# Mixer of a two-layer fp32 trunk: v by seven block products between the pieces of u, the head norm in 512-column operations, the norm of v queued early

## The chip, the cores and the metric

The kernel runs on one core of a Trainium2 chip. The core has a matrix engine (PE), three engines for elementwise work (DVE, ACT, POOL), queues for DMA transfers (SP's queue issues most of them, POOL's the accumulating ones), on-chip memory for operands and a second on-chip memory of banks into which PE accumulates. The metric is the device time of one execution in microseconds; lower is better.

## What is computed

```python
for l in range(2):                                    # D = 1024, T = 256 tokens, all in fp32
    x = LN(alpha * x + 0.5 * swiglu_1(x))
    u, v, q, k, val, gates = split(x @ w_in[l])
    u, v = gelu(u), gelu(v)                           # exact gelu
    h_a = u * spatial(LN(v))                          # per channel group: 128x128 causal mixing of positions, + bias
    o   = (softmax(q1 k1) - lam * softmax(q2 k2)) val # differential attention, 8 heads, rotary q and k
    h_b = rms_norm_per_head(o) * (1 - lam_init)
    m   = sigmoid(g_A) * (h_a @ w_branch[0]) + sigmoid(g_B) * (h_b @ w_branch[1])
    x = LN(alpha * x + m @ w_out)
    x = LN(alpha * x + 0.5 * swiglu_2(x))
```

## The kernel before

**Products in three parts.** A tile is 128 partitions wide, so the 256 tokens are two token tiles and D is eight steps of 128. Each fp32 factor is split into a high part (rounded, written by ACT) and a low part (the factor less its high part, written by DVE), and each product is three matmuls: high by high, high by low, low by high. The names are `whi`/`wlo` for weights, `xh`/`xl` (`x_cat`) for activations, `hb` for the attention's output. `stream` (L195 the high part, L197 the low) fetches a megabyte of weights through SP into one of four raw buffers and splits it in pieces of 128x1024; each piece lives in one of eight high and one of eight low buffers. `pieces`/`split` (L247, L249) do the same for data that is already there. `gemm_b` and `gemm_b2` give token rows, 512 columns a matmul (L283); `gemm_a2` gives channel rows (L295 for the high weights, 512 wide, L302 for the low ones, 256 wide), and DVE joins its two halves (L303 on ACT, L305 or L307 on DVE).

**Seven products.** In the FFN a product of 2x2 blocks is done by seven block products in place of eight (the Strassen-Winograd scheme). This needs sums of blocks of x (`strassen_sums`) and sums of weight blocks: `plus` adds two weight blocks on DVE (L359), `gather` adds a block to one in memory by an accumulating DMA from POOL's queue (L353), `homes` is a pair of the eight weight buffers used as landing place, and `product` issues the twelve matmuls of one block product (four steps of 128, three parts each, L376).

**The mixer.** In each layer, in PE's order: val (`gemm_b2`), four pairs of q and k with the rotary turn, the attention of head pair 0 to 3 (`attend`, strung in between as tasks), the gates by rows and by columns twice, `u_part((0, 1))` (two megabytes of u's weights, one 512-column gelu each), v (`gemm_b` twice, 96 matmuls of L283), `u_part((2, 3))`, the branch of `hb` (`branch_rows(1, hb)`), the spatial mixing (`spatial`, L1169), the branch of `ha`, and the output product.

At the end of `attend`, PE multiplies by val (L1049, L1051), ACT copies the bank (`on`, L1054) and sums the squares of each of four head rows (L1059), POOL works out four reciprocal roots in a chain of fifteen small operations (L1062, then `rsqrt4`, L268 to L276), ACT scales the four pieces (L1068), POOL separates the two 16-bit planes (L216) for a transposing DMA, DVE joins them (L229), and ACT and DVE write `hb`'s two parts (L1083, L1085).

v's chunks pass a gelu (ACT L1136) and `bn_stats` (DVE L1137); `settle` aggregates (L1142), takes a reciprocal root on DVE (`rsqrt`, L255 to L261) and normalizes `vg` in two operations for each half (L1146, L1148).

**What sets the order.** PE's order is the order in which the program is written. For the other engines a scheduler sorts by a priority that goes up with every fetch (`step`), so that an operation runs in the order of the fetches around it unless `soon()` lowers its number or `behind` names an instruction after which it has to be issued. Tasks (`beside(task, delay)`) are taken up after a delay counted in pieces of PE work (`beat`). `line` holds an engine's instructions to the order in which they were written, where it is set. Each engine then carries out its list strictly in order: an instruction that waits holds up all behind it.

## Time and profile before

| | |
|---|---|
| three timed runs | 1186.97, 1187.22, 1188.16 us (median 1187.22) |
| profiled execution, its own time | 1187.5 us |
| its span (first to last instruction) | 1185.8 us |
| PE / DVE / ACT / POOL busy | 1180.3 / 1013.8 / 827.9 / 280.1 us |
| granted PE clock | 1.0 throughout |

The profile has a page (busy time by engine, slices, the chain of work that ended last, the costliest groups), and the trace behind it answers with a timeline, with busy time by stretch, with waits and with groups of instructions. Rows read: start in us, duration in us, engine, line of the program, operation, output<-input, and in brackets the time for which the engine stood idle before, with what released it. Times in the text for the stage of interest are of layer 0; layer 1 shows the same rows 586.7 us later.

### The profile page before, as it was taken

What the parts mean: (1) busy time and instruction counts of PE and PEld (TensorE: products, weight loads), DVE (VectorE), ACT (ScalarE), POOL (GpSimd) and SP (SyncE); (2) the same over time, 40 slices, a digit from 0 to 9 for tenths busy, and PEclk for the clock granted to TensorE, in tenths of its full rate; (3) what the DMA queues carried; (4) which work ended last, traced back from release to release, by engine and by line L of the source; (5) the groups of instructions that cost most, each with busy time, mean ns of one, the idle gap of its engine ahead of it and who ended that gap; (6) DMA issues with size and microseconds to landing.
All of it is one profiled execution on the core that took longest, in us unless ns stands there. A gap on an engine that the chain in (4) does not pass through costs nothing.

```text
span 1185.8 us, 16672 instructions
## 1 busy us (share of the span) xinstructions
PE 1180.3 (100%) x5775; PEld 994.8 (84%) x5775; DVE 1013.8 (85%) x1559; ACT 827.9 (70%) x1418; POOL 280.1 (24%) x352
## 2 busy tenths in 40 slices
PE   9999999999999999999999999999999999999998
PEld 8888888888888888888888888888888888888887
DVE  6989989888688989889899889888965989988895
ACT  6688658559855667876567876666788556679761
POOL 1011201247420220051020141004564012102600
PEclk9999999999999999999999999999999999999999
DMA  9969976767865658689668689586666755786881
GB/s 351 260 207 262 288 272 210 264 191 239 244 210 169 225 187 273 188 275 275 229 224 262 194 274 277 198 293 231 215 203 204 255 178 172 256 247 211 271 256 36
DMA packets 129620, 275.10 MB, mean 232 GB/s; under 512 B 89040, under 2 KB 90368, under 8 KB 105472
## 3 DMA queue, kind: packets, MB, share of 16 engines
q1 hardware_dynamic: 121968, 248.67, 63.5%
q0 software_dynamic: 6992, 24.71, 8.8%
q8 instruction: 45, 0.74, 0.3%
q10 hardware_dynamic: 576, 0.66, 0.2%
q14 instruction: 39, 0.32, 0.1%
HBM read 248.05 MB, written 1.05 MB: 210 GB/s over the span
## 4 chain that ended last, share of the span: by engine, by line
PE 99%; DMA 0%; DVE 0%; ACT 0%; DVEq 0%; issue 0%
PE bank L283 46%; PE bank L295 15%; PE sbank L376 12%; PE bank L410 10%; PE bank L302 8%; PE sbank L410 3%; PE bank L521 2%; PE sbank L995 1%; PE bank L376 1%; PE sbank L1051 1%; PE sbank L1169 1%; DMA xtok<-in_xT 0%; PE sbank L1049 0%; PE sbank L692 0%; DVE xtok L679 0%; ACT whi L247 0%
## 5 line engine op out<-in xcount | busy, mean ns | idle before, releaser
L197 DVE TENSOR_TENSOR wlo<-raw,whi 128x1024 fp32r<-128x1024 f32 (+1 forms) x346 | 379.7, 1124 | 50.9 <-ACT whi L195 37.9
L195 ACT ACTIVATE whi<-raw 128x1024 fp32r<-128x1024 f32 (+1 forms) x350 | 323.2, 952 | 134.8 <-PE bank L283 43.5
L283 PE MATMUL bank<-whi,x 128*128 128x512 f32 x1224 | 386.3, 390 | 0.0
L283 PEld LDWEIGHTS bank<-whi,x 128*128 128x128 f32 x1224 | 229.9, 188 | 47.4
L283 PE MATMUL bank<-wlo,x 128*128 128x512 f32 x612 | 238.4, 390 | 0.0
L249 DVE TENSOR_TENSOR wlo<-raw,whi 128x1024 fp32r<-128x1024 f32 (+1 forms) x124 | 144.3, 1189 | 19.8 <-ACT whi L247 11.2
L247 ACT ACTIVATE whi<-raw 128x1024 fp32r<-128x1024 f32 (+1 forms) x124 | 121.6, 999 | 50.5 <-DVE raw L359 19.2
L295 PE MATMUL bank<-x,whi 128*128 128x512 f32 x640 | 153.3, 391 | 0.0
L295 PEld LDWEIGHTS bank<-x,whi 128*128 128x128 f32 x640 | 118.2, 188 | 23.7
L283 PEld LDWEIGHTS bank<-wlo,x 128*128 128x128 f32 x612 | 115.0, 188 | 23.4
L229 POOL COPY seven<-seven 128x512 uint16<-128x512 uint16 x16 | 51.9, 3299 | 139.3 <-DMA seven<-seven 80.2
L302 PEld LDWEIGHTS bank<-x,wlo 128*128 128x128 f32 x640 | 81.4, 191 | 2.9
L302 PE MATMUL bank<-x,wlo 128*128 128x256 f32 x640 | 82.6, 283 | 0.0
L410 PE MATMUL bank<-whi,hhi 128*128 128x512 f32 (+1 forms) x182 | 68.2, 375 | 0.0
L410 PE MATMUL bank<-whi,hlo 128*128 128x512 f32 (+1 forms) x182 | 67.9, 373 | 0.0
L410 PE MATMUL bank<-wlo,hhi 128*128 128x512 f32 (+1 forms) x182 | 67.9, 373 | 0.0
L971 POOL TENSOR_TENSOR swap<-swap,sin_t 128x512 f32<-128x512 f32 x16 | 28.7, 1792 | 100.9 <-DMA swap<-z 52.3
L735 POOL COPY nvia<-ntwo 128x256 uint16<-128x256 uint16 x20 | 9.9, 541 | 162.2 <-DMA ntwo<-nvia 115.2
L303 ACT ACTIVATE r<-bank 128x256 f32<-128x256 f32 x96 | 34.8, 372 | 16.2 <-PE bank L302 16.0
L376 PE MATMUL sbank<-whi,xhs 128*128 128x512 f32 x128 | 42.0, 389 | 0.0
L410 PEld LDWEIGHTS bank<-whi,hlo 128*128 128x128 f32 x182 | 34.3, 188 | 6.1
L410 PEld LDWEIGHTS bank<-wlo,hhi 128*128 128x128 f32 x182 | 34.3, 189 | 6.0
(283 smaller groups left out, 2153.5 us busy)
## 6 DMA issues: line engine op xcount, KB each, us to landing
raw<-in_w13b SPq DMA_DIRECT2D x68, 1024.0 KB, 5.7
raw<-in_w SPq DMA_DIRECT2D x32, 1024.0 KB, 7.0
raw<-in_wb SPq DMA_DIRECT2D x16, 1024.0 KB, 5.4
raw<-in_wqk SPq DMA_DIRECT2D x16, 1024.0 KB, 5.9
home<-in_w13b SPq DMA_DIRECT2D x16, 512.0 KB, 5.9
raw<-in_w13a SPq DMA_DIRECT2D x8, 1024.0 KB, 5.0
home<-in_w SPq DMA_DIRECT2D x16, 512.0 KB, 4.5
raw<-in_wgr SPq DMA_DIRECT2D x8, 1024.0 KB, 5.4
```

The source lines that it names most:

```text
L195: inline(A, A.activation(h, r, AF.Copy).ins)
L197: low = eng.tensor_tensor(out=w, in0=r, in1=h.bitcast(F32), op=ALU.subtract).ins
L229: eng.tensor_copy(out=o, in_=i)
L247: a = A.activation(hi, src, AF.Copy).ins
L249: return a, eng.tensor_tensor(out=lo, in0=src, in1=hi.bitcast(F32), op=ALU.subtract).ins
L283: PE.matmul(ps, xx, w, start=start and n == 0, stop=stop and n == 2)
L295: PE.matmul(b[-1], hi[:, k * P : (k + 1) * P], xc(k), start=k == 0, stop=False)
L302: PE.matmul(b[n][:, :T], lo[:, k * P : (k + 1) * P], xc(k)[:, :T], start=False, stop=k == KT - 1)
L303: emptied[0] = A.activation(r[:, s], b[n][:, T:], AF.Copy, scale=scale).ins
L376: PE.matmul(ps, x[o](k), y, start=start and k == n == 0, stop=stop and k == 3 and n == 2, skip_group_check=True)
L410: PE.matmul(q[c][t][:, :n] if o == 0 else more[:, :n], x(k, t), y, start=k == 8 and m == 0 and (c, t) != (1, 0), stop=k == FT - 1 and m == ...
L971: turned_by[0] = G.tensor_tensor(out=s3, in0=s3, in1=s, op=ALU.mult).ins
```

## The change

```diff
+        x_sums = []                                            # right after val's product
+        wide = [[p.tile([P, HC], F32R, tag=n, name=name("xhs")) for p, n in ((hi_pool, "hi"), (lo_pool, "lo"))] for _ in range(2)]
+        made = [[v[:, n % 2 * 512 : n % 2 * 512 + 512] for v in wide[n // 2]] for n in range(4)]
+        for _ in strassen_sums(x_sums, made, *(norm.rows[v] for v in ((0, 0), (1, 0), (0, 1), (1, 1)))):
+            pass
...
-            for q in range(4):                                 # attend: the norm of a head pair
-                A.activation(d1[:, s], on[:, s], AF.Square, accum_out=ss[:, q : q + 1])
+            A.activation(d1, on, AF.Square)
+            with behind(added[0]):
+                V.tensor_reduce(out=ss, in_=d1.rearrange("p (q c) -> p q c", q=4), op=ALU.add, axis=AX.X)
...
-            for q in range(4):
-                with behind(emptied[0]):
-                    A.activation(on[:, s], on[:, s], AF.Copy, scale=r[:, q : q + 1])
+            with behind(added[0]):
+                V.tensor_tensor(out=on4, in0=on4, in1=r.unsqueeze(2).to_broadcast([P, 4, P]), op=ALU.mult)
...
-        u_part((0, 1))
-        for h in range(2):
-            gemm_b(wb[l, V_, h], KT, xh, xl, got_v)            # 2 x 48 matmuls
+        def seven():
+            r1 = fetch(w11); p1 = pieces(r1)
+            r4 = fetch(w21); p2 = pieces(r4)
+            product(bx, x11, p1, True, False)
+            product(bq, x12, p2, True, True)
+            A.activation(cross, bx, AF.Copy)
+            r2 = fetch(w12, raw=homes(hi_pool, "hi"))
+            yield
+            product(bz, x_sums[0], pieces(plus(r1, r2)), True, False)
+            gather(r2, w22)
+            r3 = fetch(w22, raw=homes(lo_pool, "lo"))
+            V.tensor_tensor(out=vg[0][:, 0], in0=bq, in1=cross, op=ALU.add)
+            got_v(0, 0)
+            A.activation(vg[1][:, 1], bz, AF.Copy)
+            yield
+            p1 = pieces(plus(r1, r3)); p2 = pieces(r3)
+            product(bx, x_sums[1], p1, False, False)
+            A.activation(vg[0][:, 1], bx, AF.Copy)
+            product(bz, x_sums[3], p2, False, True)
+            product(bx, x_sums[2], pieces(r2), False, False)
+            plus(r1, r4)
+            V.tensor_tensor(out=vg[0][:, 1], in0=bz, in1=vg[0][:, 1], op=ALU.subtract)
+            got_v(0, 1)
+            yield
+            p1 = pieces(r1)
+            V.tensor_tensor(out=vg[1][:, 1], in0=vg[1][:, 1], in1=bx, op=ALU.subtract)
+            got_v(1, 1)
+            product(bx, x22, p1, False, True)
+            got_v(1, 0, bx)
+            yield
+        line[:] = None, None, True
+        products = seven()
+        for gp in range(GROUPS // 2):
+            u_part((gp,))
+            next(products)
+        line[:] = None, None, False
...
         def settle():                                          # the same operations, in one go
+            with soon():
...
-        beside(settle(), 2.6)
+        beside(settle(), 0.4)
         for gp in range(GROUPS // 2):
-            beside(spatial(gp), 7.4 + 1.1 * gp)
-        u_part((2, 3))
+            beside(spatial(gp), 4.2 + 1.1 * gp)
```

v is done by seven products of a quarter of the weights (84 matmuls in place of 96) that stand between the four pieces of u: u0, w11, w21, u1, the sum w11+w12, u2, three products, u3, the last product. Three sums of weights are made by DVE and one by an accumulating DMA. The sums of x are made straight after val's product into two high and two low weight buffers, which they hold until v is done. The head norm's squares become one ACT operation and one reduction on DVE, its scaling one DVE operation, behind which the engine waits for POOL's roots. `settle` is queued early and without breaks.

How the lists move, at three places (numbers behind names count the tiles; the ones of the two kernels differ). DVE, where u0's product is done and the first v weights came before; the names are `hb`, the attention output, `onT`, its transposed planes, and `nwy`, POOL's roots:

```order
L305 TENSOR_TENSOR u_3080<-bank_3091,r_3127 128x256 [waits Activation_49]
L305 TENSOR_TENSOR u_3080<-bank_3118,r_3127 128x256 [waits Activation_49]
L197 TENSOR_TENSOR wlo_3368<-raw_3361,whi_3367 128x1024
L197 TENSOR_TENSOR wlo_3404<-raw_3401,whi_3403 128x1024 [waits DMAHW2_49,PE_49,Activation_49]
L305 TENSOR_TENSOR u_3172<-bank_3183,r_3202 128x256 [waits Activation_49]
L305 TENSOR_TENSOR u_3172<-bank_3192,r_3202 128x256 [waits Activation_49]
```

```order
L305 TENSOR_TENSOR u_3090<-bank_3101,r_3135 128x256 [waits DMAHW7_49,Activation_49]
L305 TENSOR_TENSOR u_3090<-bank_3126,r_3135 128x256 [waits Activation_49]
L229 COPY onT_3053<-on_2850 128x512 [waits DMAHW3_49,DVE_49,Pool_49]
L229 COPY onT_3053<-on_2850 128x512
L1076 TENSOR_TENSOR on_3117<-on_3117,nwy_3164 128x512 [waits Pool_49]
L197 TENSOR_TENSOR wlo_3238<-raw_3235,whi_3237 128x1024 [waits DMAHW7_49,Activation_49]
L197 TENSOR_TENSOR wlo_3242<-raw_3235,whi_3241 128x1024 [waits Activation_49]
L1093 SCALAR_TENSOR_TENSOR hb_1946<-onT_3053,dgs,hb_1946 128x256 [waits Activation_49]
L1093 SCALAR_TENSOR_TENSOR hb_1947<-onT_3053,dgs,hb_1947 128x256 [waits Activation_49]
L359 TENSOR_TENSOR raw_3184<-raw_3184,home_3230 128x1024 [waits DMAHW4_49]
L359 TENSOR_TENSOR raw_3184<-raw_3184,home_3231 128x1024 [waits DMAHW5_49]
```

Before, u1's last low piece (wlo_3368; its first stands ahead of these rows) and v's first one (wlo_3404) follow u0's join at once; now the pieces of v's first two products stand ahead of these rows, the scaling that waits for POOL's roots stands between, and behind it u1's low pieces (wlo_3238, wlo_3242) and the first sum of weights.

ACT, at the same place:

```order
L1054 ACTIVATE on_3107<-sbank_3100 128x512 [waits PE_49]
L1059 ACTIVATE d_2729,ss_3109<-on_3107 128x128 [waits Activation_49]
L1059 ACTIVATE d_2729,ss_3109<-on_3107 128x128 x3
L195 ACTIVATE whi_3367<-raw_3361 128x1024 [waits PE_49]
L303 ACTIVATE r_3127<-bank_3091 128x256 [waits PE_49]
L303 ACTIVATE r_3127<-bank_3118 128x256 [waits PE_49]
L1129 ACT_TABLE_LOAD
L1129 ACTIVATE u_3080<-u_3080 128x512 [waits DVE_49]
```

```order
L1063 ACTIVATE on_3117<-sbank_3110 128x512 [waits PE_49]
L1066 ACTIVATE d_2743<-on_3117 128x512 [waits Activation_49]
L303 ACTIVATE r_3135<-bank_3101 128x256 [waits PE_49]
L303 ACTIVATE r_3135<-bank_3126 128x256 [waits PE_49]
L1052 ACTIVATE aT_2972<-d_2970 128x512 [waits DMAHW2_49,Pool_49]
L1052 ACTIVATE aT_2972<-d_2970 128x512
L1137 ACT_TABLE_LOAD
L1137 ACTIVATE u_3090<-u_3090 128x512 [waits DVE_49]
L1159 ACTIVATE cross_3183<-sbank_3180 128x512 [waits PE_49]
L195 ACTIVATE whi_3237<-raw_3235 128x1024 [waits DMAHW7_49]
L195 ACTIVATE whi_3241<-raw_3235 128x1024
```

u1's high pieces (both done before u0's gelu in the first list) now come behind u0's gelu and the copy of the first v product.

DVE at the end of the stage, up to the first low piece of `branch_rows(1, hb)` (wlo_3705 before, wlo_3604 now):

```order
L229 COPY onT_3427<-on_3304 128x512
L1148 SCALAR_TENSOR_TENSOR vg_3224<-vg_3224,nwy_3553,bc_3077 128x512 [waits DMASW1_49,DVE_49]
L1085 SCALAR_TENSOR_TENSOR hb_1934<-onT_3427,dgs,hb_1934 128x256 [waits Activation_49]
L1085 SCALAR_TENSOR_TENSOR hb_1935<-onT_3427,dgs,hb_1935 128x256 [waits Activation_49]
L1148 SCALAR_TENSOR_TENSOR vg_3224<-vg_3224,nwy_3553,bc_3077 128x512
L261 TENSOR_SCALAR nwy_3636<-nwa_3635,yi_3632 128x1
L197 TENSOR_TENSOR wlo_3705<-raw_3702,whi_3704 128x1024 [waits DMAHW2_49]
```

```order
L249 TENSOR_TENSOR wlo_3555<-raw_3184,whi_3554 128x1024
L261 TENSOR_SCALAR nwy_3639<-nwa_3638,nwy_3635 128x1 [waits DVE_49]
L1180 TENSOR_TENSOR vg_3087<-vg_3087,sbank_3180 128x512
L260 TENSOR_SCALAR nwa_3642<-nwy_3639,ve_3630 128x1 [waits DVE_49]
L229 COPY onT_3467<-on_3325 128x512 [waits DMAHW3_49,Pool_49]
L261 TENSOR_SCALAR nwy_3643<-nwa_3642,nwy_3639 128x1 [waits DVE_49]
L229 COPY onT_3467<-on_3325 128x512
L1204 SCALAR_TENSOR_TENSOR vg_3086<-vg_3086,nwy_3643,bc_3083 128x512 [waits DMASW1_49,DVE_49]
L1204 SCALAR_TENSOR_TENSOR vg_3086<-vg_3086,nwy_3643,bc_3083 128x512
L1151 BN_STATS vst_3089<-vg_3087 128x6 [waits Activation_49]
L1093 SCALAR_TENSOR_TENSOR hb_1950<-onT_3467,dgs,hb_1950 128x256 [waits Activation_49]
L1093 SCALAR_TENSOR_TENSOR hb_1951<-onT_3467,dgs,hb_1951 128x256 [waits Activation_49]
```

The next row of the changed list is wlo_3604. Between wlo_3238 and wlo_3604, both counted, the changed list has 60 instructions: 17 low pieces, 6 halves of sums of weights, 6 halves of u, 6 of `hb`, 3 sums into `vg`, one reduction, one scaling, 3 `bn_stats`, 4 copies of `onT`, and `settle` for the first token tile (13).

64 lines of the change are left out of this document (38 added, 26 removed).

## Prediction

> **What bounds the kernel now.** First the page's busy times and the waits of PE, the engine that is busy throughout:
>
> ```profile
> PE 1180.3 (100%) x5775; PEld 994.8 (84%) x5775; DVE 1013.8 (85%) x1559; ACT 827.9 (70%) x1418; POOL 280.1 (24%) x352
> PE sbank L533 <- DVE warm L529: 1.0, 1, 1.0
> PE sbank L671 <- ACT minus L669: 0.7, 1, 0.7
> PE bank L521 <- ACT whi L247: 0.3, 1, 0.3
> ```
>
> PE waits 2.0 us in all: the kernel is as long as its matmuls, and one matmul less is time gained, as long as the others still deliver in time. So the question is their slack in the stage that changes, u and v. The chain of waits gives PE's part of it, the table by stretches DVE's (the columns are stretch and length, then busy us and instructions of PE, weight loads, DVE, ACT and POOL, clock, DMA share, GB/s):
>
> ```profile
> 300.56 1.84 PE bank L295 x8
> ...
> 307.49 3.65 PE bank L295 x16
> ...
> 313.05 6.83 PE bank L283 x30
> ...
> 321.22 14.98 PE bank L283 x66
> ...
> 347.30 9.55 PE bank L283 x42
> 300.00:310.00 10.00, 10.00 (x61) 8.89 (x60) 7.30 (x10) 9.94 (x24) 3.63 (x7) 1.00 1.10 281
> 310.00:320.00 10.00, 10.00 (x55) 8.61 (x54) 6.08 (x9) 9.23 (x18) 4.31 (x13) 1.00 0.75 280
> 320.00:330.00 10.00, 10.00 (x51) 8.47 (x51) 5.08 (x9) 5.35 (x17) 4.33 (x15) 1.00 0.45 138
> 330.00:340.00 10.00, 10.00 (x47) 8.32 (x46) 8.79 (x15) 7.79 (x11) 3.99 (x7) 1.00 0.69 159
> 340.00:350.00 10.00, 10.00 (x60) 8.87 (x59) 10.00 (x27) 5.57 (x11) 0.84 (x1) 1.00 0.70 290
> ```
>
> The stage runs from 300.6 (u0) to 347.3, where the branch of `hb` begins. DVE is busy 37.3 of the 50 us, and fully so in the last ten. It has some 13 us to give.
>
> **The change part by part.**
>
> *PE.* The 96 matmuls of v take 6.83 + 14.98 = 21.81 us, 0.227 each. Seven products need 84: 12 x 0.227 = 2.73 us less in each layer, 5.5 us in all. Were nothing late, the branch would begin at 344.6.
>
> *DVE's additions.* Six more low pieces, six halves of weight sums, three sums into `vg`, two reductions and two scalings fall into the stage. The prices:
>
> ```profile
> 202.85 5.76 DVE L197 TENSOR_TENSOR wlo<-raw,whi 128x1024 fp32r<-128x1024 f32 x5
> 208.53 0.75 DVE L307 SCALAR_TENSOR_TENSOR z<-bank,r 128x256 f32<-128x256 f32 x2
> L359 DVE TENSOR_TENSOR raw<-raw,home 128x1024 f32<-128x1024 f32 x32 | 38.5, 1217 | 0.0
> L305 DVE TENSOR_TENSOR u<-bank,r 128x256 f32<-128x256 f32 x16 | 6.3, 417 | 0.4 <-ACT r L303 0.4
> L229 DVE COPY onT<-on 128x512 uint16<-128x512 uint16 x16 | 6.4, 455 | 1.5 <-DMA on<-onT 1.5
> L1085 DVE SCALAR_TENSOR_TENSOR hb<-onT,dgs,hb 128x256 fp32r<-128x256 f32 x16 | 8.2, 550 | 6.8 <-ACT hb L1083 6.8
> L1137 DVE BATCH_NORM_STATS2 vst<-vg 128x6 f32<-128x512 f32 x8 | 5.5, 690 | 7.8 <-ACT vg L1136 7.8
> L1146 DVE SCALAR_TENSOR_TENSOR vg<-vg,mv,bc 128x512 f32<-128x512 f32 x8 | 6.1, 767 | 0.0
> L843 DVE TENSOR_TENSOR held<-held,held 128x512 f32<-128x512 f32 x16 | 11.0, 686 | 0.0
> L260 DVE TENSOR_SCALAR nwa<-nwy,ve 128x1 f32<-128x1 f32 x28 | 7.6, 272 | 0.7
> ```
>
> Back to back, five low pieces take 208.53 - 202.85 = 5.68, 1.14 each against 1.22 from start to end: neighbours overlap by 0.08, which I take off every mean. A half of a sum has the same mean (1.217), so 1.14 too; a 512-column sum costs 0.61. The reduction and the scaling have no row; between half of a 512-column operation (0.34) and a whole one with its end (0.69) I take 0.6. The additions are 12 x 1.14 + 3 x 0.61 + 4 x 0.6 = 17.9 us, more than the 13 that are free, and `settle`, which before ran on past 350, now falls into the stage for its first token tile. DVE becomes the bound here.
>
> *How long it holds up the branch.* `branch_rows(1, hb)` cannot go past its first matmul without wlo_3604. DVE reaches it after 60 instructions from wlo_3238 on: 23 of 1.14 (26.2), six halves of u at 0.34 (2.0), six of `hb` at 0.47 (2.8), three sums (1.8), reduction and scaling (1.2), three `bn_stats` at 0.61 (1.8), four copies at 0.38 (1.5), four normalizations at 0.69 (2.8), nine small ones at 0.06 to 0.2 (1.2). Sum 41.3 us. When does it begin? wlo_3238 needs its high piece from ACT:
>
> ```profile
> 304.93 0.58 ACT L1054 ACTIVATE on<-sbank 128x512 f32<-128x512 f32 x1
> 307.68 0.62 ACT L303 ACTIVATE r<-bank 128x256 f32<-128x256 f32 x2
> 308.32 1.28 ACT L1129 ACT_TABLE_LOAD   x1
> 309.62 0.63 ACT L1129 ACTIVATE u<-u 128x512 f32<-128x512 f32 x1
> 313.37 1.43 ACT L1043 ACTIVATE aT<-d 128x512 uint16<-128x512 uint16 x2
> L195 ACT ACTIVATE whi<-raw 128x1024 fp32r<-128x1024 f32 x268 | 275.6, 1052 | 86.2 <-PE bank L295 30.8 <-PE bank L283 23.4 <-PE bank L410 9.5
> ```
>
> In the new order these come after u0's last matmul (u1 begins at 307.5, as before): r until about 308.0, `aT` 1.4, table 1.3, gelu 0.5, the copy `cross` 0.5, the high piece 1.05: 312.7. The other wait ahead of it, for POOL's roots, ends earlier, as below. DVE has next to nothing to do from 308.5 until then. 312.7 + 41.3 = 354.0. Against that stands the matmul that first reads such a low piece:
>
> ```profile
> 347.37 0.40 PE L283 MATMUL bank<-wlo,hb 128*128 128x512 f32 x1
> ```
>
> It comes 354.0 - 347.4 = 6.6 us later, although PE had 2.7 us less to do.
>
> *POOL's chain.* The last head pair's scaling on DVE waits for fifteen small POOL operations, and these fare badly beside a busy DVE:
>
> ```profile
> 327.66 0.20 POOL L273 TENSOR_TENSOR nwa<-nwy 128x4 f32<-128x4 f32 x1
> 327.93 0.20 POOL L274 TENSOR_TENSOR nwa<-nwa,ve 128x4 f32<-128x4 f32 x1
> 1091.86 15.07 POOL L229 COPY seven<-seven 128x512 uint16<-128x512 uint16 x1
> 1093.58 4.63 DVE L197 TENSOR_TENSOR wlo<-raw,whi 128x1024 fp32r<-128x1024 f32 x4
> 1106.67 1.28 DVE L249 TENSOR_TENSOR wlo<-raw,whi 128x1024 fp32r<-128x1024 f32 x1 [0.37 <-ACT whi L247]
> ```
>
> Undisturbed, an operation of the chain follows the one before by 0.28 us, fifteen in 4.2. But a POOL copy begun while DVE went from one sum of two arrays to the next took 15.07 us and ended at 1106.9, just past DVE's first gap (1106.3 to 1106.67). For the first chain here DVE mostly idles, hence no delay to the 312.7. For the second one DVE has ten operations (about 9 us) between reduction and scaling; POOL gets on during `bn_stats`, u's two halves and the copies, some 2.4 us or eight operations, and DVE then stands for the other seven: 7 x 0.28 = 2.0 us. Bounds: 0 (all fifteen pass) and 4.2. The Trainium skill, "SBUF — State Buffer", section "Who interferes with whom", states that a DVE instruction with two SBUF inputs shuts out a GpSimd one that reads SBUF for its whole length; the row of 15.07 us agrees. The rule speaks against this change: without it the term would be 0.
>
> *Behind the stage.* The second token tile's `settle` now follows wlo_3604 and the pieces behind it, and the spatial matmuls of `ha` come within 10 us. Bounds 0 and 1.5 us from the four normalizations (2.8) against 1.2 us of slack; I take 0.5.
>
> *At nothing.* The sums of x are eight DVE operations of 0.61 (4.9 us) ahead of q's first low pieces, which are read by the first L302 of q:
>
> ```profile
> 199.44 2.36 DVE L197 TENSOR_TENSOR wlo<-raw,whi 128x1024 fp32r<-128x1024 f32 x2
> 206.04 1.91 PE bank L302 x16
> ```
>
> The first piece was done at 199.44 + 1.22 = 200.7 and is now by 205.6 at the latest, 0.4 before 206.0. If that cover fails it costs up to 1 us in each layer. The four weight buffers that they hold lower the run ahead from eight pieces to six; the gate stage, where DVE has idle time, covers that. SP and POOL issue four transfers more each; DMA's share of its engines is 0.45 to 0.75 from 310 on, where they fall. ACT gains six high pieces and loses the short operations of the head norm; it was busy 5.4 and 7.8 of 10 us between 320 and 340, so but for its order it is not the bound.
>
> **Sum.** For each layer 6.6 + 2.0 + 0.5 = 9.1 us, and both layers have the same lists: 18.2. From the profiled execution's own 1187.5 (span 1185.8 and 1.7 around it; the median of the runs is 1187.22) that makes 1205.7; as the terms' bounds leave more room below, I say 1205. By bounds: 6.6 less 2 if all rows shrink by 5%, no wait for POOL, nothing behind: 4.6, so 1197; and 6.6 + 4.2 + 1.5 = 12.3, so 1212.
>
> **The rivals.**
>
> *DVE keeps up and PE stays the bound:* 1187.5 - 5.5 = 1182. For it: DVE idles 13 us of 50, and before 300 it can run ahead. Against: from wlo_3238 the 41 us would have to fit into the 32 from 312.7 to 344.6, each row 22% shorter. Only if that piece could start at 303 would it fit, and ACT's list forbids that.
>
> *DVE loses only what it has too much of:* if ACT's pieces come some 5 us sooner (table and `aT` copies out of the way) and POOL does not hold it up, the branch starts at 348 to 350: +1 to +3 for each layer, 1189 to 1194. For it: ACT is full from 300 to 310 (9.94 of 10), and the head norm takes some of that away. Against: its order, in which the six instructions ahead of the piece all depend on u0's end.
>
> *POOL starves DVE further:* the transposed planes of the last head pair pass through two POOL copies while DVE is full. If one of them waits 15 us as at 1091.86, the transfer and the join behind it (a DVE row before wlo_3604) come some 5 to 6 us late: 1205 + 11 = 1216. Against: `bn_stats` and the sums from banks leave POOL two openings there.
>
> **How the numbers follow.** The main case 0.62, with 1197 to 1212 as its own range; PE-bound 0.10; the small loss 0.13; the starved POOL 0.15. About 0.2% (2.4 us) is what a measurement can tell from no change. Faster: the PE-bound case and a little of other errors, 0.11. Same: the lower edge of the small loss, 0.04. Slower 0.85. Leaving out the PE-bound case and the end of the starved one, the range is 1188 to 1214.
>
> **What would show it.** In the changed profile PE should wait about 11 to 12 us in each layer between 330 and 365, mostly for DVE's low pieces, the longest wait (5 to 9 us) at the start of the branch of `hb`; DVE should be busy without a gap from about 313 to 355, but for about 2 us before the last scaling, released by POOL; and between 308 and 313 it should stand for ACT. PE's busy time should be 5.5 us lower. I am wrong if PE's waits are at other stages, if DVE has gaps in that stretch, or if wlo_3604 is in time.

## The result, and the profile after

| | before | after |
|---|---|---|
| median of four runs each, on the same chip | 1187.51 us | 1214.69 us |
| from to | 1186.97 to 1188.16 | 1213.55 to 1215.99 |
| ratio | | 1.0228, 95% interval 1.0216 to 1.0241 |
| profiled execution / span | 1187.5 / 1185.8 | 1215.7 / 1213.9 |

The change makes the kernel 27 us slower. The forecast was 1205 with a range up to 1214, so the sign held, and the loss was larger than the range allowed, by 0.7 us. The profiled execution, 1215.7 us, lies 1.0 above the median. The page's busy times of the changed kernel:

```profile
PE 1186.8 (98%) x5751; PEld 993.5 (82%) x5751; DVE 1067.2 (88%) x1621; ACT 831.4 (68%) x1356; POOL 307.0 (25%) x356
```

PE has 24 matmuls fewer (5.5 us) and is yet busy 6.5 us longer. The lower clock below accounts for about 5 of these 12 us (an estimate: PE's busy time in the slow stretches of both layers, times the share of the clock that is missing there); the rest was not traced. Its waits (engine, output, line, what it waited for; us in total, times, longest):

```profile
PE sbank L376 <- DVE wlo L249: 8.8, 8, 2.1
PE sbank L376 <- DVE vg L1180: 4.8, 1, 4.8
PE sbank L376 <- ACT whi L195: 4.1, 1, 4.1
PE bank L283 <- DVE wlo L197: 1.7, 3, 0.8
...
PE sbank L1058 <- issue: 1.0, 1, 1.0
...
PE bank L283 <- DVE gz L305: 0.5, 1, 0.5
```

The first four rows are the new stage in both layers (19.4 us), where there was nothing before. The third row is layer 1's counterpart of the second: the profile names ACT there, but in both layers PE goes on 0.15 us after the same subtraction of DVE (L1180) has ended, at 356.17 and at 955.56. Busy time by stretch in layer 0 (columns as in the prediction):

```profile
300.00:310.00 10.00, 10.00 (x65) 9.03 (x64) 8.33 (x12) 7.52 (x17) 6.59 (x6) 1.00 0.81 161
310.00:320.00 10.00, 10.00 (x50) 8.38 (x49) 6.59 (x11) 7.81 (x14) 3.51 (x15) 1.00 0.41 124
320.00:330.00 10.00, 8.42 (x48) 6.78 (x47) 9.36 (x11) 7.20 (x11) 3.35 (x5) 1.00 0.99 278
330.00:340.00 10.00, 9.69 (x50) 7.71 (x48) 8.49 (x12) 8.63 (x13) 8.75 (x15) 1.00 0.78 164
340.00:350.00 10.00, 7.21 (x33) 5.74 (x34) 10.00 (x11) 5.82 (x7) 5.10 (x7) 1.00 0.60 131
350.00:360.00 10.00, 5.15 (x21) 4.20 (x21) 9.17 (x22) 6.25 (x10) 1.50 (x1) 0.75 0.85 310
```

From 320 on DVE is busy nearly throughout, and PE, which was busy throughout before, falls to 5.15 of 10 us. DVE's list in the timeline, from the scaling ahead of wlo_3238 (the first low piece of u1) to wlo_3604 (the first one of the branch of `hb`, the first half of the row at 361.02):

```profile
315.59 0.69 DVE L1076 TENSOR_TENSOR on<-on,nwy 128x512 f32<-128x512 f32 x1 [3.25 <-POOL nwy L276]
316.20 2.36 DVE L197 TENSOR_TENSOR wlo<-raw,whi 128x1024 fp32r<-128x1024 f32 x2
...
323.50 1.90 DVE L249 TENSOR_TENSOR wlo<-raw,whi 128x1024 fp32r<-128x1024 f32 x1
...
328.86 0.69 DVE L1068 TENSOR_REDUCE ss<-d 128x4 f32<-128x512 f32 x1 [0.59 <-ACT d L1066]
...
339.94 0.69 DVE L1076 TENSOR_TENSOR on<-on,nwy 128x512 f32<-128x512 f32 x1 [1.51 <-POOL nwy L276]
...
341.69 1.58 DVE L1093 SCALAR_TENSOR_TENSOR hb<-onT,dgs,hb 128x256 fp32r<-128x256 f32 x2
...
351.39 1.06 DVE L1202 SCALAR_TENSOR_TENSOR vg<-vg,mv,bc 128x512 f32<-128x512 f32 x1
...
358.87 0.69 DVE L1151 BATCH_NORM_STATS2 vst<-vg 128x6 f32<-128x512 f32 x1 [0.39 <-ACT vg L1150]
360.22 0.89 DVE L1093 SCALAR_TENSOR_TENSOR hb<-onT,dgs,hb 128x256 fp32r<-128x256 f32 x2 [0.65 <-ACT hb L1091]
361.02 2.35 DVE L197 TENSOR_TENSOR wlo<-raw,whi 128x1024 fp32r<-128x1024 f32 x2
```

Three rows are longer than their kind elsewhere: a low piece takes 1.90 in place of 1.22, two operations of `hb` 1.58 in place of 0.88, a normalization 1.06 in place of 0.74. Two of these three share their time with a copy of POOL (L216), the third with POOL's operation on `wsT`:

```profile
315.36 0.20 POOL L276 TENSOR_TENSOR nwy<-nwa,nwy 128x4 f32<-128x4 f32 x1
...
322.81 1.50 POOL L216 COPY onT<-on 128x512 uint16<-128x512 uint16 x2
329.63 1.10 POOL L1071 TENSOR_TENSOR ss<-s,ss 128x4 f32<-128x4 f32 x1 [5.32 <-DVE ss L1068]
...
339.71 0.20 POOL L276 TENSOR_TENSOR nwy<-nwa,nwy 128x4 f32<-128x4 f32 x1
340.77 2.23 POOL L216 COPY onT<-on 128x512 uint16<-128x512 uint16 x2 [0.86 <-DVE on L1076]
...
350.40 1.50 POOL L1213 TENSOR_SCALAR_AFFINE_SELECT wsT<-wsT 128x512 f32<-128x512 f32 x1 [3.23 <-DMA wsT<-in_sguwT]
```

POOL's second chain of fifteen operations runs from 329.63 to 339.91, 10.3 us in place of 4.2 undisturbed. PE before the stage, at the last product and at the branch (the row at 362.29 is the matmul that the prediction put at 356.0):

```profile
203.34 0.50 PE L295 MATMUL bank<-x,whi 128*128 128x512 f32 x1 [0.26 <-ACT whi L195]
...
262.12 0.46 PE L1058 MATMUL sbank<-val,d 128*128 128x128 f32 x2 [0.96 <-issue]
...
278.43 0.50 PE L283 MATMUL bank<-whi,x 128*128 128x512 f32 x1 [0.53 <-DVE gz L305]
...
356.32 0.77 PE L376 MATMUL sbank<-whi,x 128*128 128x512 f32 x1 [4.85 <-DVE vg L1180]
...
362.29 0.50 PE L283 MATMUL bank<-wlo,hb 128*128 128x512 f32 x1 [0.21 <-DVE wlo L197]
```

**Where the 27 us lie.** By the same matmuls in the two traces, after less before: head pair 0's product with val in layer 0 +2.3; first low piece of the branch read 362.29 - 347.37 = +14.9; output product +16.2; head pair 0 in layer 1 +15.9; low piece of the branch 961.21 - 934.07 = +27.1; output product and end +27.5. So layer 0 loses 2.3 ahead of the stage's neighbourhood, 12.6 up to the branch and 1.3 behind it; layer 1 loses 11.2 and 0.4.

### The profile page after: what moved, and what is told of

It is laid out like the page before. It is cut to its first block, busy times and chain, and to the rows that moved or that the text cites. A ratio compares the mean times of both kernels' runs of the same rounds, so it can differ in the third digit from the quotient of the medians.

```text
span 1213.9 us, 16657 instructions
## 1 busy us (share of the span) xinstructions
PE 1186.8 (98%) x5751; PEld 993.5 (82%) x5751; DVE 1067.2 (88%) x1621; ACT 831.4 (68%) x1356; POOL 307.0 (25%) x356
## 3 DMA queue, kind: packets, MB, share of 16 engines
HBM read 250.15 MB, written 1.05 MB: 207 GB/s over the span
## 5 line engine op out<-in xcount | busy, mean ns | idle before, releaser
L197 DVE TENSOR_TENSOR wlo<-raw,whi 128x1024 fp32r<-128x1024 f32 (+1 forms) x330 | 363.7, 1131 | 23.1 <-ACT whi L195 21.8
L283 PE MATMUL bank<-whi,x 128*128 128x512 f32 x1096 | 346.2, 390 | 0.5 <-DVE gz L305 0.5
L283 PEld LDWEIGHTS bank<-whi,x 128*128 128x128 f32 x1096 | 205.7, 188 | 43.5 <-DVE gz L305 0.7
L283 PE MATMUL bank<-wlo,x 128*128 128x512 f32 x548 | 213.3, 389 | 0.0
L247 ACT ACTIVATE whi<-raw 128x1024 fp32r<-128x1024 f32 (+1 forms) x144 | 142.1, 1007 | 65.4 <-DVE raw L359 40.4
L249 DVE TENSOR_TENSOR wlo<-raw,whi 128x1024 fp32r<-128x1024 f32 (+1 forms) x144 | 170.5, 1206 | 17.7 <-ACT whi L247 9.4
L283 PEld LDWEIGHTS bank<-wlo,x 128*128 128x128 f32 x548 | 102.9, 188 | 21.0
L376 PE MATMUL sbank<-whi,xhs 128*128 128x512 f32 x192 | 64.2, 397 | 0.0
L376 PE MATMUL sbank<-whi,x 128*128 128x512 f32 x144 | 50.2, 413 | 9.0 <-DVE vg L1180 4.8
L359 DVE TENSOR_TENSOR raw<-raw,home 128x1024 f32<-128x1024 f32 x40 | 49.2, 1243 | 0.5 <-DMA home<-in_w13b 0.5
L376 PE MATMUL sbank<-wlo,xhs 128*128 128x512 f32 x96 | 39.1, 408 | 8.8 <-DVE wlo L249 8.8
```

The source lines that it names most:

```text
L197: low = eng.tensor_tensor(out=w, in0=r, in1=h.bitcast(F32), op=ALU.subtract).ins
L247: a = A.activation(hi, src, AF.Copy).ins
L249: return a, eng.tensor_tensor(out=lo, in0=src, in1=hi.bitcast(F32), op=ALU.subtract).ins
L283: PE.matmul(ps, xx, w, start=start and n == 0, stop=stop and n == 2)
L359: inline(V, V.tensor_tensor(out=v, in0=v, in1=m, op=ALU.add).ins)
L376: PE.matmul(ps, x[o](k), y, start=start and k == n == 0, stop=stop and k == 3 and n == 2, skip_group_check=True)
```

## Experiments

Theory D is that of the prediction: DVE's list from u1's first low piece to the branch's first one, work and waits, sets the end of the stage. The rivals are named in each expectation. Ratios are to the kernel before, with their 95% intervals.

### The head norm: back in the changed kernel, and alone in the old one

```diff
-            A.activation(d1, on, AF.Square)
-            V.tensor_reduce(out=ss, in_=d1.rearrange(...), op=ALU.add, axis=AX.X)
+            for q in range(4): A.activation(d1[:, s], on[:, s], AF.Square, accum_out=ss[:, q : q + 1])
...
-            V.tensor_tensor(out=on4, in0=on4, in1=r..., op=ALU.mult)
+            for q in range(4): A.activation(on[:, s], on[:, s], AF.Copy, scale=r[:, q : q + 1])
```

> The changed kernel with the head norm as before: four squares with their sums and four scalings on ACT, no reduction and no scaling on DVE. Theory D (VectorE's list from u1's first low piece to the branch's first one sets the stage, work and waits alike): inside the stage VectorE loses two operations (1.2 us) and two waits, for ACT's squares (0.59) and for POOL's roots (1.51), so the branch starts about 3.3 us sooner in each layer: 1214.7 - 6.6 = 1208. If POOL's roots ahead of u1's pieces (a wait of 3.25) count too, up to 5 us in each layer: 1205. Rival P (PE's wait of 4.8 us before the last product, for the subtraction that empties its bank, and the slow clock behind it, set the end): that subtraction stands 3 us sooner too, the same sign but at most 3 us. Rival N (the head norm is the whole loss): back to about 1187.

Measured: 1211.87 us, 1.0207 (1.0190 to 1.0224); 2.8 us better than the change, where theory D had 6.6. All four runs lie below the change's four, though the two intervals still touch.

The second run is the kernel before with the new head norm alone (the same edit the other way round).

> The kernel before with the head norm in 512-column operations and nothing else. Theory D: in the kernel before VectorE has about 13 us idle in this stage, so its waits for POOL's roots are hidden: 1187 to 1190. Rival N: the waits of about 7 us in each layer show by themselves: 1195 to 1201.

Measured: 1188.09 us, 1.0005 (0.9995 to 1.0014). Where DVE has idle time the head norm on it costs nothing; beside the rest of the change it costs 2.8. Undoing it frees four 512-column operations of DVE (2.4 us a layer) and two waits, and brings less than that, because POOL's roots are then waited for by ACT, in front of a high piece that DVE needs. From the timelines of ACT and of DVE in the first run:

```profile
336.99 0.99 ACT L1077 ACTIVATE on<-on,nwy 128x128 f32<-128x128 f32 x3 [2.66 <-POOL nwy L276]
```

```profile
339.73 1.32 DVE L249 TENSOR_TENSOR wlo<-home,whi 128x1024 fp32r<-128x1024 f32 x1 [3.40 <-ACT whi L247]
```

### v's norm not queued early

```diff
-            with soon():
-                for t in range(NT):
-                    V.bn_aggr(out=mvs[t], in_=vst[t])
...
+            for t in range(NT):
+                mv = sm("mv", 2)
+                V.bn_aggr(out=mv, in_=vst[t])
...
+                    yield 1
```

> The changed kernel with the norm of v queued as before (not early, with its breaks). Theory D: thirteen rows (about 4.5 us) leave VectorE's list ahead of the branch's first low piece, so the branch starts 4 to 5 us sooner in each layer, and the spatial products wait for the norm, which gives back 0 to 4 of it: 1206 to 1214. Rival S (the norm's place costs nothing, since what leaves the list in front is waited for behind it): 1213 to 1216.

Measured: 1229.0 us, 1.0342 (1.0325 to 1.0360), 14 us worse than the change and above both forecasts. PE's timeline shows the price behind the branch:

```profile
379.30 1.65 PE L1223 MATMUL sbank<-wsT,vg 128*128 128x128 f32 x6 [7.14 <-DVE vg L1202]
```

So the early queueing, which puts thirteen instructions onto the crowded part of DVE's list, is still the better place: the same work in the old order makes PE wait 7.1 us at the spatial matmuls.

### DVE's work taken away

The sums of weights left out: the pieces are made of one block each, so v is not the reference's.

```diff
-            product(bz, x_sums[0], pieces(plus(r1, r2)), True, False)
+            product(bz, x_sums[0], pieces(r1), True, False)
...
-            p1 = pieces(plus(r1, r3))
+            p1 = pieces(r1)
...
-            plus(r1, r4)
```

> The changed kernel without its three sums of weights on VectorE (the products read the plain blocks, so v comes out wrong); nothing else is left out. Theory W: VectorE loses 6 x 1.14 = 6.8 us between u1's first low piece and the branch in each layer, all of it on the path: 1214.7 - 13.7 = 1201. Theory B: the start of that list stays at 316, and since VectorE then keeps up with PE from u2 on, the gain ends where PE is the bound again: a gain of 3 to 6 us in each layer, 1203 to 1209, with VectorE's idle time at 308 to 316 unchanged.

Measured: 1205.26 us, 1.0145 (1.0130 to 1.0161): 9.4 us gained in two layers, of the 12 x 1.14 = 13.7 us that are taken off DVE. No other edit gained as much. The time lies in the range of theory B (1203 to 1209), but not by its mechanism: PE is not the bound again, it still waits for DVE ahead of the last product (2.4 us) and at the branch (2.2). Some of the rest stays in a new wait. DVE's timeline in that run:

```profile
314.17 2.35 DVE L197 TENSOR_TENSOR wlo<-raw,whi 128x1024 fp32r<-128x1024 f32 x2
...
329.54 1.23 DVE L249 TENSOR_TENSOR wlo<-home,whi 128x1024 fp32r<-128x1024 f32 x1 [1.54 <-ACT whi L247]
...
350.66 0.69 DVE L1151 BATCH_NORM_STATS2 vst<-vg 128x6 f32<-128x512 f32 x1 [2.03 <-ACT vg L1150]
...
353.38 1.22 DVE L197 TENSOR_TENSOR wlo<-raw,whi 128x1024 fp32r<-128x1024 f32 x1
```

From u1's first low piece to the branch's first one it is 39.2 us against 361.02 - 316.20 = 44.8 in the change. Now a `bn_stats` that stands ahead of the branch's pieces waits for a gelu of ACT. It is that of the quarter of v whose subtraction (L1179 here, done at 347.5) empties the last product's bank; in ACT's list a high piece of the branch and u3's gelu stand in front of it:

```profile
348.53 1.06 ACT L195 ACTIVATE whi<-raw 128x1024 fp32r<-128x1024 f32 x1 [2.88 <-DVE onT L229]
349.50 0.61 ACT L1137 ACTIVATE u<-u 128x512 f32<-128x512 f32 x1
350.01 0.61 ACT L1150 ACTIVATE vg<-vg 128x512 f32<-128x512 f32 x1
```

So ACT's list is next behind DVE's.

The roots of the last two head pairs left out (fourteen of POOL's fifteen operations; `hb` is not scaled as in the reference):

```diff
-            r = rsqrt4(ss, 1.0 / (2 * HD))
+            r = rsqrt4(ss, 1.0 / (2 * HD)) if hp < 2 else ss
```

> The changed kernel without POOL's reciprocal roots for head pairs 2 and 3 (they are scaled by the sums themselves, so the output is wrong): fourteen of the fifteen POOL operations of those two chains are left out, VectorE's list is unchanged. Theory L (POOL's roots hold VectorE: waits of 3.25 and 1.51 us in each layer, the first one partly covered by ACT's pieces of u1, which come 0.8 us before it ends): the branch starts 1.5 to 3 us sooner in each layer: 1209 to 1212. Rival (all of it is covered by other waits, above all ACT's and the raw buffers'): 1213 to 1216. If the roots were the whole of VectorE's lag: below 1206.

Measured: 1210.23 us, 1.0193 (1.0178 to 1.0208): 4.5 us gained. The start of DVE's list hardly moved, since the wait for POOL became one for ACT:

```profile
314.85 2.36 DVE L197 TENSOR_TENSOR wlo<-raw,whi 128x1024 fp32r<-128x1024 f32 x2 [3.00 <-ACT whi L195]
```

What went is the second chain and its wait of 1.51 us: to 358.30, the start of the branch's first piece, it is 43.45 us in place of 44.8. About 1 us more was gained ahead of the stage, where the runs differ anyway. The two runs together say that DVE's list sets the end, and that POOL's roots are part of it.

The sums of x left out (blocks of x stand in for them, and the four weight buffers that they hold are free):

```diff
-        for _ in strassen_sums(x_sums, made, *(norm.rows[v] for v in ((0, 0), (1, 0), (0, 1), (1, 1)))):
-            pass
...
-            product(bx, x_sums[1], p1, False, False)
+            product(bx, x12, p1, False, False)
```

> The changed kernel without the sums of x: the four products that read them read blocks of x instead, so v comes out wrong, while every product, piece and sum of weights stays. It leaves out eight VectorE and four ACT operations near 200 us and frees the two high and two low weight buffers that the sums hold. Theory B (buffers: of eight, the sums hold two and the landing places of w12 and w22 two, so u1's pieces cannot be made before the first product of v has released w11's, and VectorE idles until 316): u1's pieces are made before u0 ends, as in the kernel before, 5 to 8 us sooner in each layer, and the loss ahead of the stage in layer 0 (2.7 us) goes: 1196 to 1203. Theory W (only VectorE's work counts): the sums' work lies outside the stage, so only the 2.7 us go: 1211 to 1213.

Measured: 1218.45 us, 1.0259 (1.0244 to 1.0274), worse than the change and outside both forecasts, although DVE has less to do. What stood ahead of the stage went: head pair 0's product with val came 0.1 us later than before, not 2.3, and the two waits of PE at 203.3 and 262.1 are gone. In u3 DVE was 6 us ahead, and then stood:

```profile
351.58 0.42 DVE L305 TENSOR_TENSOR u<-bank,r 128x256 f32<-128x256 f32 x1 [4.50 <-ACT r L303]
```

because in ACT's list a high piece of the branch, without its weights yet, stands in front of u3's r:

```profile
350.22 1.06 ACT L195 ACTIVATE whi<-raw 128x1024 fp32r<-128x1024 f32 x1 [5.94 <-DMA raw<-in_wbrr]
351.19 0.36 ACT L303 ACTIVATE r<-bank 128x256 f32<-128x256 f32 x1
```

### The sums of weights by accumulating transfers

All three instead of DVE's additions, and in a second run the last one only:

```diff
-            p1 = pieces(plus(r1, r3))
+            p1 = pieces(gather(r1, w22))
...
-            plus(r1, r4)
+            gather(r1, w21)
```

> The changed kernel with its three sums of weights made by accumulating transfers in place of VectorE (so all four sums are made by transfers). Theory D: VectorE loses 6 x 1.14 = 6.8 us of work between u1's first low piece and the branch in each layer; if the transfers land in time the branch starts that much sooner: 1214.7 - 13.7 = 1201. Rival Q (POOL's queue is then the bound, since its accumulating transfers wait for VectorE's low pieces and stand ahead of the root chains): no gain or a loss, 1212 to 1225, with VectorE waiting for POOL longer than 4.8 us in each layer. Rival P: no change, 1214.

Measured: 1245.45 us, 1.0488 (1.0472 to 1.0504). DVE is freed of 13.7 us, and the kernel loses 31 more, beyond even rival Q's 1225. POOL's and DVE's timelines:

```profile
326.16 0.91 POOL L353 DMA_DIRECT2D home<-in_wb  x1 [11.47 <-DMA home<-in_wb]
...
345.95 0.86 POOL L353 DMA_DIRECT2D raw<-in_wb  x1 [13.63 <-DVE wlo L249]
```

```profile
322.09 0.79 DVE L229 COPY onT<-on 128x512 uint16<-128x512 uint16 x2 [10.96 <-DMA on<-onT]
...
344.42 1.23 DVE L249 TENSOR_TENSOR wlo<-raw,whi 128x1024 fp32r<-128x1024 f32 x1 [10.42 <-ACT whi L247]
```

POOL stands 11 to 14 us before it can issue a transfer, and the copies of the planes and the roots stand behind it.

> The changed kernel with only the last sum of weights (w21 added to what the first raw buffer holds) made by an accumulating transfer, so that w21's raw buffer is free some 35 us sooner and VectorE has 2.3 us less to do. Theory R (raw buffers: w11 and w21 hold two of four until the last sum, and the branch's second megabyte is fetched only then, at 346.7, and awaited by ACT for 2.9 us ahead of `hb`): the branch's weights are there early, ACT's wait goes, and with the 2.3 us the branch starts 3 to 5 us sooner in each layer: 1205 to 1209. Theory W (VectorE's work only): 2.3 us in each layer: 1210. Rival Q (the accumulating transfer itself is late, as where all three were transfers): 1214 to 1225, with ACT waiting for it ahead of the last product's pieces.

Measured: 1227.49 us, 1.0331 (1.0314 to 1.0349), above every forecast. The transfer was issued at 340.1; ACT began the pieces of its two halves at 346.46 and 349.72, the second after a wait of 2.2 us for it, and then stood 6.1 for a raw buffer's next weights, ahead of the gelu and `hb`. Combined with the old head norm, and with w12 in a raw buffer of its own:

> The changed kernel with the head norm as before and the last sum of weights by an accumulating transfer. If the two add up, the gain of the norm undone (2.8 us in all) comes on top of that of the last sum: 1202 to 1207 by theory R. If ACT, which then carries the norm again, is what waits at the end, no better than the last sum alone.

Measured: 1223.16 us, 1.0301 (1.0286 to 1.0317).

> Both of the last: w12 in a raw buffer (two high buffers more) and the last sum by an accumulating transfer (a raw buffer less). Theory B+R (weight buffers at the start and raw buffers at the end are two limits, and each change alone moved the wait to the other): u1's pieces come 3 us sooner as where w12 alone went to a raw buffer, and the branch's weights are not late: 1203 to 1208, better than either alone. Rival: no better than the last sum by transfer alone.

Measured: 1222.62 us, 1.0297 (1.0282 to 1.0312). Neither comes near the change itself.

### The bank of the last product, and the buffers

The subtraction that empties the bank (L1180) put ahead of the last pieces on DVE:

```diff
+            V.tensor_tensor(out=vg[1][:, 1], in0=vg[1][:, 1], in1=bx, op=ALU.subtract)
             got_v(0, 1)
+            got_v(1, 1)
             yield
             p1 = pieces(r1)
-            V.tensor_tensor(out=vg[1][:, 1], in0=vg[1][:, 1], in1=bx, op=ALU.subtract)
-            got_v(1, 1)
```

> The changed kernel with one operation moved: the subtraction that empties the last product's bank (and the gelu and statistics of that block) stands ahead of u3's low pieces, where the bank is ready. Theory D: the last product no longer waits 4.8 us for it, but only for its low piece (about 2.5 us), and PE then waits as much longer at the branch, whose first low piece comes after the same work: no change, 1213 to 1216. Rival P: the branch starts sooner by the wait and the slow clock, 4.8 to 7 us in each layer: 1201 to 1205.

Measured: 1218.35 us, 1.0258 (1.0243 to 1.0273), above theory D's 1213 to 1216. The wait of 4.85 us for the bank turned into one of 4.15 for the last product's low piece: the bank is not the limit, DVE is. On the way DVE lost 1.89 us in a wait for ACT's r of u3, which stands behind a high piece of the branch that waited 3.14 us for its weights.

w12 fetched into a raw buffer in place of two high weight buffers (`fetch(w12)`):

> The changed kernel with w12 landing in a raw buffer in place of two high buffers; all else as it is. Theory B: two more high buffers let u1's high pieces be made before u0 ends, so VectorE starts on them when a low buffer comes free (u0's end, about 311) or sooner, 3 to 5 us sooner in each layer, less what a raw buffer less costs: 1204 to 1210. Theory W: the same work in the same order, 1213 to 1216, or slower for want of a raw buffer.

Measured: 1221.65 us, 1.0283 (1.0267 to 1.0298); with one raw buffer fewer for the branch, a high piece of it waits 5.55 us for its weights on ACT, and DVE 4.0 us for the r of u3 that stands behind it.

A fifth raw buffer, its place taken from four of 26 activation buffers, with the control that only loses those four:

```diff
-RAW, HL = 4, 8
+RAW, HL = 5, 8
...
-    act = ctx.enter_context(tc.tile_pool(name="act", bufs=26))
+    act = ctx.enter_context(tc.tile_pool(name="act", bufs=22))
```

> The changed kernel with a fifth raw buffer for weights (its place taken from four of the 26 512-column activation buffers). Theory D (DVE's list of work and waits from u1's first low piece to the branch's first one sets the stage, ACT's fetches arrive before DVE gets there): nothing on DVE's list changes, 1213 to 1217. Theory R (the raw buffers that the stage holds until the last sum make ACT's list late, and that is a second limit already now): the 2.9 us that ACT waits for the branch's raw buffer and the waits of DVE for ACT behind it go, 1209 to 1212.

> Control for the fifth raw buffer: the changed kernel with 22 in place of 26 activation buffers and still four raw ones. All theories: 1214 to 1217; if the FFNs need the four buffers, more, and then the runs with five raw buffers are to be compared with this one.

Measured: 1218.68 us, 1.0266 (1.0250 to 1.0281) with five; 1220.44 us, 1.0280 (1.0265 to 1.0296) for the control. The control was expected at 1217 at most. Its extra time is a new wait at the spatial matmuls, where the tables come later because of the missing buffers:

```profile
PE sbank L1225 <- POOL wsT L1213: 5.5, 2, 2.9
```

Against the control the buffer is worth 1.8 us by the medians, and the intervals overlap.

> Five raw buffers and the three sums of weights on DVE left out (v's columns come out wrong). With four raw buffers this gave 1205.3, 9.4 less than the changed kernel, where 13.7 us of DVE work were taken away. Theory D: the rest is a smaller overlap of DVE's operations, so a fifth buffer adds nothing: 1204 to 1206. Theory R: the missing 4 us went into ACT's late pieces: 1200 to 1202.

Measured: 1206.68 us, 1.0164 (1.0147 to 1.0181), not better than with four raw buffers (1205.26). It pays for the four lost activation buffers too, though less than the control (PE waits 1.5 us for `wsT`), so a gain of one or two microseconds by the fifth buffer is not excluded.

> Five raw buffers and the sums of x left out (v comes out wrong), so that the four weight buffers they hold are free. With four raw buffers this gave 1218.5: DVE was 6 us ahead in u3 and then stood for ACT, whose list had the branch's high piece, waiting for a raw buffer, ahead of u3's r. Theory R: that wait goes and the 6 us stay in both layers: 1202 to 1206. Theory D, or a wait in ACT's list that is not for the raw buffer: 1214 to 1219.

Measured: 1216.45 us, 1.0245 (1.0229 to 1.0260). By its number theory R misses (1202 to 1206), yet the mechanism that it names is there: DVE's 4.50 us for r are gone from the trace, and DVE gets 6 us further ahead. It then stands for the gelu of the last product, whose `bn_stats` is ahead of the branch's first low piece in this run:

```profile
355.28 0.69 DVE L1145 BATCH_NORM_STATS2 vst<-vg 128x6 f32<-128x512 f32 x1 [1.82 <-ACT vg L1144]
```

The branch's low piece was read at 357.16, 5.1 us earlier than in the change (2.4 of them gained ahead of the stage), and part of this is lost again behind it (PE waits 0.7 for `wsT`, 0.8 for `ha`). Raw buffers are a second limit, behind DVE's list.

### PE kept busy in its waits

```diff
+            for _ in range(64):
+                PE.matmul(bq[:, :P], warm, warm, start=True, stop=True)
             product(bx, x22, p1, False, True)
             got_v(1, 0, bx)
+            for _ in range(36):
+                PE.matmul(bq[:, :P], warm, warm, start=True, stop=True)
```

> The changed kernel with 64 small bf16 matmuls on a constant (0.056 us each at full clock, into the idle third bank) where PE waits before the last product, and 36 where it would then wait before the branch. Nothing changes on the other engines. Theory C (what the stage loses beyond DVE's list is PE's clock, 0.50 to 0.82 from 355 to 365, that falls in these waits): the clock stays at 1.0, the last product takes 2.7 in place of 5.3 us, which the wait for the branch's low piece swallows, but the branch runs at full rate: 1.0 to 1.5 us a layer, 1211.5 to 1213. Theory D (DVE alone): 1214 to 1216.

Measured: 1218.44 us, 1.0259 (1.0245 to 1.0273). The clock by stretch in the change and then in this run (the column behind POOL's):

```profile
355.00:360.00 5.00, 3.68 (x9) 2.94 (x10) 4.17 (x10) 5.00 (x7) 0.00 (x0) 0.50 0.71 236
```

```profile
355.00:360.00 5.00, 5.00 (x55) 4.32 (x53) 4.88 (x13) 4.35 (x8) 0.00 (x0) 1.00 0.62 210
```

The last product ran at full clock (358.94 - 356.11 = 2.83 us in place of 5.3), and the branch's low piece was read at 361.64, 0.65 earlier than in the change; in layer 1 it was read 1.0 later (962.19). Nothing is gained: at the branch PE still waits for DVE's piece (0.23). But this run is no clean test of theory C, since the clock was low one step earlier than in the change: 0.68 and 0.64 from 340 to 350, where the change had 1.00. The first sixteen matmuls of u3 took 5.1 us in place of 3.6, and DVE waited 0.87 for the r behind them. Why this run is some 4 us slower than the change is not explained beyond that.

> As the run without DVE's three sums of weights (1205.3, v's columns wrong; 13.7 us of DVE work gone, 9.4 us gained), with 34 small matmuls before the last product and 30 before the branch. There PE waited 2.4 and 2.2 us, the clock was 0.81 and 0.66 from 350 to 360, and 4.1 us were lost between the branch of hb and the output product. Theory C: the clock stays at 1.0 and these become 1 to 2, 2 to 3 us a layer less: 1199.5 to 1202. Theory D (the second token tile's norm and what follows it on DVE's list make the loss behind the branch): 1204 to 1206.

Measured: 1207.03 us, 1.0164 (1.0151 to 1.0178), against 1205.26 without the small matmuls: no gain here either. In layer 0 the clock still fell, to 0.66 from 355 to 360, after a wait of 2.6 us for the branch's piece. Layer 1 is the clean test: there the clock stayed at 1.00 from 910 to 975, where it was 0.74 to 0.84 from 940 to 955 without the small matmuls. One stretch of each, without and then with them:

```profile
945.00:950.00 5.00, 2.90 (x10) 1.50 (x9) 5.00 (x9) 3.10 (x5) 0.00 (x0) 0.84 0.00 0
```

```profile
945.00:950.00 5.00, 3.75 (x40) 2.98 (x39) 4.10 (x7) 4.98 (x8) 0.00 (x0) 1.00 0.04 11
```

From head pair 0's product to the output product that layer takes 997.22 - 855.15 = 142.1 us without and 998.98 - 856.75 = 142.2 with them. So theory C falls: the slow clock lies under the wait for DVE.

No version beats the kernel before. The nearest that leave nothing out are the old kernel with the new head norm (no difference) and the change with the old head norm (1.0207).

## Why the prediction was right in kind and wrong in size

**What bounds the stage: right.** PE is no longer the bound; DVE's list is. Taking work or waits off it gained (9.4, 4.5 and 2.8 us), while emptying the bank, filling PE's waits or freeing buffers did not. Moving DVE's three sums of weights to POOL's queue cost 31 us more, so it is not enough that work leaves DVE: what takes it over must deliver in time. PE's 2.73 us of matmuls a layer are lost in the wait, as said.

**The price of DVE's work: nearly right.** The list was costed at 41.3 us of work and 2.0 of waiting, that is 41.3 - 1.14 + 2.0 = 42.2 from the start of wlo_3238 to that of wlo_3604. It took 44.8. The difference has two parts, less 0.2 by which other rows were shorter than costed. The waits were 1.51 (POOL, 2.0 predicted) and 0.59 + 0.39 + 0.65 for ACT, for which the sum had nothing: +1.1. And the three rows beside POOL's operations are longer by 0.68 + 0.70 + 0.32 = 1.7 us. **This is the term that was mis-sized:** the part on POOL's chain asked only how long POOL is shut out and DVE then waits for it, and not how long a POOL operation, once it has begun, holds DVE. It was a loss in both layers, and it goes where POOL's operation goes: with the old head norm the copies are over at 339.98 and the two operations of `hb`, at 340.97, take 0.87; without the late roots the operation on `wsT` lies beside a low piece at 347.21, which takes 1.53, and the normalization at 348.73 takes 0.73. The Trainium skill, "SBUF — State Buffer", section "Who interferes with whom", says both: that the order of issue decides who blocks. The rows agree: a copy of POOL's 2.23 us and DVE's 1.58 in place of 0.88 in the same stretch.

**When the list begins: 3.5 us late in layer 0.** It was put at 312.7 and began at 316.2. The step "At nothing" failed here: the sums of x were to be hidden, with up to 1 us as their price if not. In layer 0 PE waits 0.26 for q's first pieces, 0.96 in head pair 0's product and 0.53 at the gates, 1.75 us ahead of the stage. The first two are gone in the two runs without sums of x; the second is missing in the run without sums of weights as well, so that its tie to the sums of x is likely but not shown. The third needs the new head norm too: it is 0.15 us with that norm alone, 0.15 and 0.17 with it and no sums of x, and is not there with the old norm. Of the rest of the shift 0.7 us lie before the mixer, where nothing was changed, and 1.0 us stands without a wait that explains it. Runs with the same code up to there place head pair 0 by 0.6 to 2.3 us later than before. In layer 1 nothing was lost ahead of the stage. That the first wait for POOL ends before ACT's piece is ready was true by little: POOL 315.56, ACT 314.78 + 1.05 = 315.83. DVE's scaling still stands between the two, and without the roots the list starts 0.35 us sooner, counted from head pair 0's product (314.85 - 261.12 = 53.73 against 316.20 - 262.12 = 54.08).

**Behind the stage: 0.5 predicted, 1.3 and 0.4 measured.** The sign of this term and its place were right; without the early queueing it would have been 7.1 us at the spatial matmuls.

**The sum.** Predicted 9.1 for each layer. Layer 0: 9.1 + 3.5 (start) + 2.6 (list) + 0.8 (behind) = 16.0 against 16.2; layer 1: 9.1 + 0.3 + 2.1 - 0.1 = 11.4 against 11.3. The range's upper end took the bounds of POOL's wait and of what is behind, and no room for ACT's waits, for POOL holding DVE, or for a late start (the 1 us named under "At nothing" is not in it); that is why the time stood outside it.

**Rivals.** PE-bound (1182): out, PE waits 19.4 us in the two stages. The small loss: out, ACT's piece came with u0's end, as the argument against it said. The starved POOL gave 1216, near the time, but not by its mechanism: the copies took 1.50 and 2.23 us and not 15, and the chain of roots was the slow part (10.3 us), most of it hidden under ten DVE operations. That the number fits is chance.

**What was to be seen.** PE's waits came to 9.7 us a layer where 11 to 12 were foretold (8.2 of them between 330 and 365 in layer 0). The longest was to stand at the branch; it stands at the last product (4.85), and the branch waits 0.2 and 0.8: the low piece of the branch is late by the same list, but PE spends the time one product earlier and more slowly. PE's busy time was to fall by 5.5 and rose by 6.5, which the slower matmuls after the waits explain in part. Between 308 and 313 DVE was to stand for ACT; it stood 1.79 us for ACT and then 3.25 for POOL, up to 315.6. From there on the list has the gaps named above and no others.

## What to carry to other kernels

When a change moves work onto an engine with some idle time, lay out that engine's list from the last thing that holds it to the first thing that PE needs, and add what the waits on the other lists and the shared use of the memory by POOL add, since the summed means alone were 2.6 us short in 42. Saved matmuls are worth nothing where their factors arrive late. A buffer or a bank set free brings nothing as long as the list is the limit, and in in-order lists it moves instructions that then wait in front of others: freeing the bank, the buffers of the sums of x, or those of w12 all lost by that. ACT stood 3.1, 5.9 and 5.6 us for the branch's weights, in front of the r that DVE needed next.

## What the runs showed of the hardware

After the wait of 4.85 us PE's granted clock fell to 0.50 and the twelve matmuls of the last product took 5.25 us, 0.44 each in place of 0.227, for about five microseconds. Shorter waits were followed by a slow clock as well. In layer 1 of the change, behind a wait of 2.13 us, two matmuls took 1.05 in place of 0.63:

```profile
941.22 0.50 PE L376 MATMUL sbank<-wlo,xhs 128*128 128x512 f32 x1 [2.13 <-DVE wlo L249]
...
942.40 1.05 PE L376 MATMUL sbank<-whi,xhs 128*128 128x512 f32 x2
```

The same wait in layer 0, at 341.82, left the clock at 1.00. The Trainium skill, "TensorE: Matmul & The Clock Gate", section "HAM oscillation — how this bites in real kernels", puts the limit at gaps of about 3.4 us; the wait of 4.85 us agrees with it, the one of 2.13 us in layer 1 does not, and here the measurement decides. What else sets the clock no run here shows. The run with small matmuls in the waits held 1.00 at the last product and was slow ahead of it (0.68 and 0.64 from 340 to 350).
